# A hybrid encoder layer: three PSUM banks shared by maxima, queries and convolutions, filter taps kept in PSUM, and a modulation that only TensorE sums

## The chip, the cores and the metric

One core of a Trainium2 chip runs the whole layer as one program. The metric is the device time of one execution in microseconds (us); lower is better. TensorE, VectorE, ScalarE, GpSimd and SyncE are called PE, DVE, ACT, POOL and SP, as in the profile.

## The reference, cut to what matters

The layer works on 2048 positions of width 1024 in fp32. Four pieces matter here:

```
mod = silu(c) @ w_ada + b_ada                    # six vectors of 1024: shift, scale, gate, twice
u = x * (1 + sc1) + sh1;  proj = u @ w_in        # feeds attention (8 heads) and the Hyena group
s = q k^T;  p = softmax(s * scale);  o = p v     # per head, 2048 x 2048, no mask
h = (hid @ w3 + b3) * exp(-t * |decay|)          # taps of the two long filters, 2 x 512 channels
y = irfft(rfft(z) * rfft(h))                     # two long convolutions, each followed by a gate
```

The two groups are normalised, joined and multiplied by `w_o`; sixteen SwiGLU experts follow. Matrix products that must be exact to fp32 are made of three fp32r products (`mm3`: high x high, high x low, low x high), so most operands exist as a high part (`hi_of`) and a remainder (`lo_of`).

## The kernel before, in words

The program is written stage by stage, and a scheduler of the compiler orders the instructions of each engine within what data and buffers allow. A buffer pool gives each name a fixed number of buffers; an allocation beyond that number waits until an earlier one has been read for the last time. The PSUM has eight banks of 128 x 512 fp32, and `Banks` hands them out by tag.

Filters (0 to about 240 us). `modulation` loads `w_ada` in sixteen tiles of 128 x 1024 (`w`, five buffers). The first half of the columns is summed over the eight row blocks by PE (L158); of the second half, blocks 0 to 4 are multiplied and added by POOL (L161 to L165), and one product with ones (L170) adds up that sum. `hidden` computes the filters' small network: per block of 512 positions a product, five DVE operations that reduce a sine's argument (L98 to L102), and a sine. `taps(o, q)` then makes 64 tiles of filter taps: `mm3` into a bank of tag `a`, DVE adds the bias and writes SBUF (L307), POOL multiplies by the decay `e` (L308), ACT and DVE split the product (L59 and L65, tile `h`). A second `mm3` per tile (tag `b`) is the first step of the filter's transform. Beside it `ahead` modulates the first half of the input (`inputs`, tiles `ut` and `uT`, L370 to L372) and starts the input projection (tag `mm`).

Projections (240 to 608 us) follow, with the other four modulation vectors, made by DVE in between.

Attention with convolutions (608 to 1900 us). `attention` goes through 32 blocks (8 heads x 4 blocks of 512 queries) of 16 steps. A step makes the scores of 128 keys (tag `s`, three products, L887 to L889), two exponentials by ACT (L892, L893), a remainder by DVE (`el`), a running sum by POOL (L901), and two products with the values (L874, L875, tags `o` and `l`). In the same steps, the maxima of the next block are made: a product of tag `x` (L815) and a DVE reduction (L817), sixteen times; then the row of maxima goes through PE as four transposes (L829, from tile `mz`) and by ACT into the query tile (L830). Only then can the next block's scores start. Queries (`query`) also use tag `x`.

Beside the attention runs `beside`: the values and the keys of the other heads, and then `hyena`, the two long convolutions, in tasks `fwd1` (L652), `spectrum` (L667), `mid` (L694 and L715) and `inv` (L736). All of them use tag `h`, one bank. A credit in the loop at L974 sets how many steps of `beside` are written per step of attention; what is left is written behind it (L979). The bank of one `mid` product is read three times: by DVE (L698) and twice by ACT (L700, L701).

The output projection starts with `prep(0)`: it loads one tile of the attention's output (`at`), one of the convolutions' (`hy`), and the eight tiles of `w_o`, all by SP's queue, whose instructions go in order.

Of the kernel before, what the change touches and what calls it, by code (L numbers as in the profile page):

```python
# [43 lines left out]
def pat(ap, offset, dims):  # L44
    return bass.AP(tensor=ap.tensor, offset=ap.offset + offset, ap=[list(d) for d in dims])
# [3 lines left out]
def hybrid_layer(ctx, tc, I, out):  # L49
# [97 lines left out]
    def modulation(wp, bk, b2):  # L147
        A.activation(sc, vc("c", 0, 8), AF.Silu)
        ps = [bk("sm"), bk("mm"), b2("b"), b2("b")]
        acc = [None, None]  # L150
        for k in range(8):
            for hh in range(2):
                w = wp.tile([128, 1024], F32, name="w")
                SY.dma_start(w, I["w_ada"][0, k * 128:(k + 1) * 128, hh * 1024:hh * 1024 + 1024])
                eng = G if hh and k <= 4 else None
                if eng is None:
                    for j in range(2):
                        T.matmul(ps[hh * 2 + j][0:1], sc[:, k:k + 1], w[:, j * 512:j * 512 + 512],  # L158
                                 start=k == 5 * hh, stop=k == 7 and hh == 0)
                elif k == 0:  # L160
                    G.tensor_scalar(w, w, sc[:, 0:1], 0.0, op0=OP.mult, op1=OP.add)  # L161
                    acc[hh] = w
                else:
                    G.tensor_scalar(w, w, sc[:, k:k + 1], 0.0, op0=OP.mult, op1=OP.add)
                    G.tensor_tensor(acc[hh], acc[hh], w, OP.add)  # L165
            yield
        for hh in range(2):
            for j in range(2):
                if acc[hh] is not None:
                    T.matmul(ps[hh * 2 + j][0:1], ones[:, 0:1], acc[hh][:, j * 512:j * 512 + 512], start=False, stop=True)  # L170
        row = [wp.tile([128, 1024], F32, name="w") for _ in range(2)]
        for j in range(4):
            o = row[j // 2][0:1, j % 2 * 512:j % 2 * 512 + 512]
            if j % 2:
                V.tensor_copy(o, ps[j][0:1])
            else:
                A.activation(o, ps[j][0:1], AF.Copy)
        p = bk("sm")
        for j in range(16):
            T.matmul(p[:, j:j + 1], row[j // 8][0:1, j % 8 * 128:j % 8 * 128 + 128], ones[0:1, 0:1], start=True, stop=True)  # L180
        V.tensor_tensor(sh1, p[:, 0:8], vc("b_ada", 0, 8), OP.add)
        V.scalar_tensor_tensor(s1, p[:, 8:16], 1.0, vc("b_ada", 8, 8), op0=OP.add, op1=OP.add)
        yield
# [41 lines left out]
    def filters(tp, wk, ht, bk):  # L225
# [3 lines left out]
        w3 = ht.tile([128, 2 * CH], F32, name="w3")  # L229
        h1 = ht.tile([128, S], F32, name="h1")  # L230
        negt = tp.tile([128, 32], F32, name="negt")
        b3 = tp.tile([128, 2 * CH], F32, name="b3")
        dec = tp.tile([128, 2 * CH], F32, name="dec")
        SY.dma_start(w1b, I["filt_w1"])
        for b in range(4):
# [6 lines left out]
        for i in range(2):  # L242
            r = slice(i * 64, i * 64 + 64)
            SY.dma_start(dec[r], pat(I["hyena_decay"], i * 1024, [[0, 64], [1, 1024]]))
            SY.dma_start(b3[r], pat(I["filt_b3"], i * 1024, [[0, 64], [1, 1024]]))
        hsh = tp.tile([128, 32, 128], F32R, name="hsh")
        hsl = tp.tile([128, 32, 128], F32R, name="hsl")
        for t in (hsh, hsl):
# [42 lines left out]
        def taps(o, q):  # L291
            oc = slice(o * CH, (o + 1) * CH)
            p = bk("a")
            mm3(p, hsh[:, q, :], hsl[:, q, :], w3h[:, oc], w3l[:, oc], True, True)
            e = wk.tile([128, CH], F32, name="e")
            ex = A.activation(e, dec[:, oc], AF.Exp, scale=negt[:, q:q + 1])
            if len(hs) < 3 and q in (2, 3):
                for d in sines:
                    tc.add_manual_dep(ex.ins, d.ins.name,
                                      mybir.DependencyInfo(mybir.DependencyClass.NoSync, mybir.DependencyReason.DATA),  # L300
                                      reason="one change of the activation table")
            if q == 0:
                hb = wk.tile([128, CH], F32, name="e")
                SY.dma_start(hb[0:1], I["hyena_bias"][0, o:o + 1])
                V.tensor_tensor(b3[0:1, oc], b3[0:1, oc], hb[0:1], OP.add)
            t = wk.tile([128, CH], F32, name="t")
            V.tensor_tensor(t, p, b3[:, oc], OP.add)  # L307
            G.tensor_tensor(t, t, e, OP.mult)  # L308
            if q == 0:
                G.memset(t[64:65, :], 0.0)  # L310
            h = wk.tile([128, 2, CH], F32R, name="h", bufs=3)
            hi_of(A, h[:, 0], t)
            lo_of(V, h[:, 1], t, h[:, 0])
            hs[o, q] = h

        for n, (layer, b) in enumerate(((0, 0), (0, 1), (1, 0), (0, 2), (1, 1), (0, 3), (1, 2), (1, 3))):
            hidden(layer, b)
            if n == 1:
                hi_of(A, w3h, w3)
                lo_of(G, w3l, w3, w3h)  # L320
            yield
        order = list(range(1, 16)) + [0]
        seq = [(o, q2 * 2 + i) for q2 in order for o in range(2) for i in (1, 0)]
# [40 lines left out]
    def inputs(b, xp):  # L364
        for f in range(0, 8, 2):
            xt = xp.tile([128, 2, 512], F32, name="xt")
            SY.dma_start(xt, I["xT"][f * 128:(f + 2) * 128, b * 512:(b + 1) * 512].rearrange("(f p) t -> p f t", p=128))
            for i in range(2):
                t = xp.tile([128, 512], F32, name="ut")
                A.activation(t, xt[:, i], AF.Identity, scale=s1[:, f + i:f + i + 1], bias=sh1[:, f + i:f + i + 1])  # L370
                hi_of(V, uT[b][0][:, f + i], t)
                last_in[0] = lo_of((V if b == 2 else G, V)[i], uT[b][1][:, f + i], t, uT[b][0][:, f + i])  # L372
            yield

    def load_w(job):
# [579 lines left out]
            yield from hyena(pool(hs_, "hc", side="right"), pool(hs_, "hcw", bufs=2, side="right"), bk)  # L955

    with ExitStack() as st:
        at_ = Banks(st, "psT", s=3, x=2, o=1, l=1)
        hb_ = Banks(st, "psH", h=1)
        weight(wk, I["w_kvb"][0])  # L960
        for i in range(2):
            G.dma_start(khs[i][64:96], KR)
        norm_kv(0, at_("x"))
        for b in range(4):
            if b < 3:
                norm_kv(b + 1, at_("x"))
            keys(b, 0, at_("s"), None)
            if b < 2:
                weight(wqs[b], I["w_qb"][0, b * 128:b * 128 + 128])
                norm_q(b, hb_("h"))  # L970
        at = attention(pool(st, "atk"), pool(st, "atw", bufs=2), at_)
        hy = beside(hb_)
        credit = 0.0
        for n, free in enumerate(at):  # L974
            credit += free * (1.5 if n < 12 else 0.8)
            while credit >= 1.0:
                credit -= 1.0
                next(hy, None)
        drive(hy)  # L979
# [748 lines left out]
```

## Time and profile before

| | us |
|---|---|
| three runs, median (lowest to highest) | 3405.52 (3395.53 to 3406.53) |
| the profiled execution, its own time | 3403.19 |
| its span in the trace | 3401.4 |
| PE busy, DVE busy, ACT busy, POOL busy | 3177.4, 2286.6, 1700.0, 1459.6 |

The span is what the trace covers; the execution's own time is 1.8 us longer. The ends of matmuls are modelled, so a busy PE is not a PE at its peak: back to back matmuls of 128 x 512 fp32r start 0.23 us apart while each is shown with some 0.39 us. PEclk is the share of full speed that was granted to TensorE.

### The profile page before, as it was taken

Reading aid. Unit: us, or ns where it says so; the run is one execution under the profiler, and the core shown is the slowest. Engines: PE = TensorE matmul, PEld = TensorE weight load, DVE = VectorE, ACT = ScalarE, POOL = GpSimd, SP = SyncE. Lnnn points to the kernel's source line nnn. Section 1 sums busy time; section 2 is a strip of 40 time slices with the busy share of each in tenths; the row PEclk is TensorE's granted clock in tenths of the full one; section 3 lists DMA queues with packets and bytes.
Section 4 is the critical chain, followed back from the end, with each engine's and each line's share of the span. In section 5 each row is a group of like instructions: output and inputs, shape, how many; then the busy total and the mean of one; then the engine's idle time right before and its main releaser. Section 6 shows DMA issues by size and latency. Waiting matters only on the chain.

```text
span 3401.4 us, 41832 instructions
## 1 busy us (share of the span) xinstructions
PE 3177.4 (93%) x14790; PEld 2466.7 (73%) x14790; DVE 2286.6 (67%) x3528; ACT 1700.0 (50%) x2569; POOL 1459.6 (43%) x1134
## 2 busy tenths in 40 slices
PE   7899999999999999999999799599999999999897
PEld 3667877667677776777777588477788878887676
DVE  7975344786677766776685577776665665665886
ACT  4662222466667666766765343243444444443443
POOL 5650000466777776777786366200100010000564
PEclk8999999699999999999999899799999999999999
DMA  6443352346575764667566543455666666665884
GB/s 195 158 155 114 106 145 81 119 148 179 147 186 144 202 158 146 156 191 197 148 161 216 199 149 118 162 187 184 210 198 198 193 222 217 198 198 186 276 278 163
DMA packets 364794, 594.14 MB, mean 175 GB/s; under 512 B 36092, under 2 KB 189246, under 8 KB 364138
## 3 DMA queue, kind: packets, MB, share of 16 engines
q1 hardware_dynamic: 338137, 528.95, 49.0%
q0 software_dynamic: 26304, 62.00, 7.4%
q8 instruction: 117, 1.92, 0.2%
q14 instruction: 92, 0.75, 0.1%
q10 hardware_dynamic: 144, 0.52, 0.0%
HBM read 438.84 MB, written 152.58 MB: 174 GB/s over the span
## 4 chain that ended last, share of the span: by engine, by line
PE 72%; DVE 11%; DMA 7%; issue 4%; POOL 3%; ACT 3%; SPq 0%; POOLq 0%; DVEq 0%; ACTq 0%
PE g L73 9%; PE g L74 9%; PE g L75 9%; PE s L887 3%; PE s L888 3%; PE mm L75 3%; PE s L889 3%; PE mm L74 3%; PE mm L73 3%; PE x L815 3%; PE o L874 3%; PE l L875 3%; DMA w<-in_w_ada_dram 2%; PE h L736 2%; PE h L652 2%
## 5 line engine op out<-in xcount | busy, mean ns | idle before, releaser
L901 POOL TENSOR_TENSOR acc<-acc,eh 128x512 f32<-128x512 f32 x480 | 615.8, 1283 | 175.9 <-ACT eh L892 155.8
L65 DVE TENSOR_TENSOR wl<-raw,wh 128x2048 fp32r<-128x2048 f32 (+1 forms) x210 | 473.0, 2255 | 224.6 <-ACT wh L59 223.5
L59 ACT ACTIVATE wh<-raw 128x2048 fp32r<-128x2048 f32 x192 | 367.6, 1915 | 440.8 <-PE g L75 337.8
L65 DVE TENSOR_TENSOR el<-s,eh 128x512 fp32r<-128x512 f32 x512 | 348.3, 686 | 175.9 <-ACT s L893 172.3
L892 ACT ACTIVATE eh<-s 128x512 fp32r<-128x512 f32 x512 | 305.1, 596 | 223.5 <-PE s L889 204.8
L817 DVE TENSOR_REDUCE mx<-x 128x1 f32<-128x512 f32 x512 | 341.1, 683 | 111.3 <-PE x L815 108.1
L73 PE MATMUL g<-wh,xh 128*128 128x512 f32 x1024 | 411.9, 403 | 1.3 <-ACT wh L59 0.7
L75 PE MATMUL g<-wh,xl 128*128 128x512 f32 x1024 | 408.2, 399 | 1.0 <-DVE xl L65 1.0
L74 PE MATMUL g<-wl,xh 128*128 128x512 f32 x1024 | 408.8, 399 | 0.0
L1527 POOL DMA_INDIRECT ACC<-ye,idx x30 | 67.9, 2263 | 687.7 <-DVE ye L1518 565.3
L893 ACT ACTIVATE s<-s 128x512 f32<-128x512 f32 x512 | 304.4, 595 | 0.0
L875 PE MATMUL l<-el,vt 128*66 128x512 f32 x512 | 230.0, 452 | 2.3 <-DVE el L65 1.9
L75 PEld LDWEIGHTS g<-wh,xl 128*128 128x128 f32 x1024 | 193.3, 189 | 45.5 <-DVE xl L65 1.4
L73 PEld LDWEIGHTS g<-wh,xh 128*128 128x128 f32 x1024 | 193.4, 189 | 44.8 <-ACT wh L59 1.1
L74 PEld LDWEIGHTS g<-wl,xh 128*128 128x128 f32 x1024 | 193.6, 189 | 43.3 <-DVE wl L65 0.4
L887 PE MATMUL s<-qt,kh 97*128 97x512 f32 x512 | 212.4, 415 | 3.0 <-ACT qt L830 2.0
L815 PE MATMUL x<-kh,qt 96*128 96x512 f32 x512 | 211.3, 441 | 3.9 <-DVE mx L817 2.4
L73 PE MATMUL mm<-uT,wh 128*128 128x512 f32 x512 | 208.1, 408 | 5.3 <-DVE uT L62 5.3
L73 PE MATMUL g<-wh,hh 128*128 128x512 f32 x512 | 206.5, 404 | 4.5 <-ACT hh L59 4.5
L74 PE MATMUL g<-wl,hh 128*128 128x512 f32 x512 | 206.3, 403 | 3.7 <-DVE wl L65 3.7
L74 PE MATMUL mm<-uT,wh 128*128 128x512 f32 x512 | 206.7, 404 | 1.1 <-DVE uT L65 0.7
L75 PE MATMUL mm<-uT,wl 128*128 128x512 f32 x512 | 205.6, 402 | 0.0
(408 smaller groups left out, 6954.6 us busy)
## 6 DMA issues: line engine op xcount, KB each, us to landing
raw<-in_w_gate_dram SPq DMA_DIRECT2D x64, 1024.0 KB, 5.2
raw<-in_w_up_dram SPq DMA_DIRECT2D x64, 1024.0 KB, 7.9
raw<-in_w_down_dram SPq DMA_DIRECT2D x64, 1024.0 KB, 9.7
tc<-F_dr SPq DMA_DIRECT2D x64, 512.0 KB, 6.6
w<-in_w_ada_dram SPq DMA_DIRECT2D x48, 512.0 KB, 4.4
Af<-ev SPq DMA_DIRECT2D x32, 512.0 KB, 2.6
Ad<-tc SPq DMA_DIRECT2D x32, 512.0 KB, 5.2
tc<-Af SPq DMA_DIRECT2D x16, 1024.0 KB, 5.6
```

What stands on the lines that cost most here:

```text
L59: return A.activation(hi, src, AF.Copy)
L65: return eng.tensor_tensor(lo, src, hi.bitcast(F32), OP.subtract)
L73: first = T.matmul(o, wh, xh, start=start, stop=False)
L74: T.matmul(o, wh, xl, start=False, stop=False)
L75: T.matmul(o, wl, xh, start=False, stop=stop)
L815: T.matmul(p, qh[0:96, i * 128:i * 128 + 128], khs[h % 2][0:96, 0, c * 512:c * 512 + 512], start=True, stop=True)
L817: V.tensor_reduce(mx[:, i, c:c + 1], p, axis=AX.X, op=OP.max)
L875: T.matmul(pl[0:66], vt[:, k, 64:130], el, start=k == 0, stop=k == NT - 1)
L887: T.matmul(p, kh[0:97, ks], qh[0:97, :], start=True, stop=False)
L892: A.activation(eh, p, AF.Exp, scale=SCALE)
L893: A.activation(p, p, AF.Exp, scale=SCALE)
L901: G.tensor_tensor(acc, acc, eh.bitcast(F32), OP.add)
```

## The change

Four edits. (1) The modulation's five POOL blocks become PE products like the others. (2) A tile of taps stays in its PSUM bank: the bias is a fourth matmul into the bank (a selecting matrix `sel` times the bias's high and low parts `b3s`), DVE multiplies by the decay in place, and the split reads the bank. (3) Of the input's remainders, all for the first two blocks of positions are made by POOL, all for the last two by DVE. (4) The tag `h` is gone: its bank goes to `x`, which has three, and convolutions, keys, values and the scales of `norm_q` take `x`.

```
@@ modulation
-        acc = [None, None]
...
-                eng = G if hh and k <= 4 else None
-                if eng is None:
-                    for j in range(2):
-                        T.matmul(ps[hh * 2 + j][0:1], sc[:, k:k + 1], w[:, j * 512:j * 512 + 512],
-                                 start=k == 5 * hh, stop=k == 7 and hh == 0)
-                elif k == 0:
-                    G.tensor_scalar(w, w, sc[:, 0:1], 0.0, op0=OP.mult, op1=OP.add)
-                    acc[hh] = w
-                else:
-                    G.tensor_scalar(w, w, sc[:, k:k + 1], 0.0, op0=OP.mult, op1=OP.add)
-                    G.tensor_tensor(acc[hh], acc[hh], w, OP.add)
+                for j in range(2):
+                    T.matmul(ps[hh * 2 + j][0:1], sc[:, k:k + 1], w[:, j * 512:j * 512 + 512], start=k == 0, stop=k == 7)
...
-                    T.matmul(ps[hh * 2 + j][0:1], ones[:, 0:1], acc[hh][:, j * 512:j * 512 + 512], start=False, stop=True)
@@ filters
+        b3s = tp.tile([128, 2 * CH], F32R, name="b3s")
+        sel = tp.tile([128, 128], F32R, name="sel")
+        G.memset(b3, 0.0)
...
-            SY.dma_start(b3[r], pat(I["filt_b3"], i * 1024, [[0, 64], [1, 1024]]))
+        for i in range(4):
+            SY.dma_start(b3[32 * i:32 * i + 1], pat(I["filt_b3"], i % 2 * 1024, [[0, 1], [1, 1024]]))
@@ taps
-            mm3(p, hsh[:, q, :], hsl[:, q, :], w3h[:, oc], w3l[:, oc], True, True)
+            mm3(p, hsh[:, q, :], hsl[:, q, :], w3h[:, oc], w3l[:, oc], True, False)
+            T.matmul(p, sel, b3s[:, oc], start=False, stop=True)
...
-                V.tensor_tensor(b3[0:1, oc], b3[0:1, oc], hb[0:1], OP.add)
-            t = wk.tile([128, CH], F32, name="t")
-            V.tensor_tensor(t, p, b3[:, oc], OP.add)
-            G.tensor_tensor(t, t, e, OP.mult)
+                V.tensor_tensor(p[0:1], p[0:1], hb[0:1], OP.add)
+            V.tensor_tensor(p, p, e, OP.mult)
             if q == 0:
-                G.memset(t[64:65, :], 0.0)
+                V.memset(p[64:65, :], 0.0)
             h = wk.tile([128, 2, CH], F32R, name="h", bufs=3)
-            hi_of(A, h[:, 0], t)
-            lo_of(V, h[:, 1], t, h[:, 0])
+            hi_of(A, h[:, 0], p)
+            lo_of(V, h[:, 1], p, h[:, 0])
@@ inputs
-                last_in[0] = lo_of((V if b == 2 else G, V)[i], uT[b][1][:, f + i], t, uT[b][0][:, f + i])
+                last_in[0] = lo_of((V if b >= 2 else G), uT[b][1][:, f + i], t, uT[b][0][:, f + i])
@@ attention and what runs beside it
-        at_ = Banks(st, "psT", s=3, x=2, o=1, l=1)
-        hb_ = Banks(st, "psH", h=1)
+        at_ = Banks(st, "psT", s=3, x=3, o=1, l=1)
+
+        def hb_(tag):
+            return at_("x")
```

On PE in the filters, this stands before in the middle of the stage (`a` is a tile of taps, `b` the transform's product, `mm` the projection):

```order
L73 MATMUL b_828<-h_778,w1h_759 128x512
L74 MATMUL mm_1743<-uT11_98,wh_529 128x512
L75 MATMUL mm_1743<-uT10_97,wl_530 128x512
L73 MATMUL a_875<-w3h_141,hsh_135 128x512
L74 MATMUL a_875<-w3l_142,hsh_135 128x512
L75 MATMUL a_875<-w3h_141,hsl_136 128x512
L74 MATMUL b_828<-h_778,w1h_759 128x512
L75 MATMUL b_828<-h_778,w1l_760 128x512
```

And in the changed kernel at a like place:

```order
L75 MATMUL b_912<-h_869,w1l_835 128x512
L73 MATMUL a_918<-w3h_151,hsh_145 128x512
L74 MATMUL a_918<-w3l_152,hsh_145 128x512
L75 MATMUL a_918<-w3h_151,hsl_146 128x512
L289 MATMUL a_918<-b3s_121,sel_122 128x512
L73 MATMUL b_930<-h_886,w1h_834 128x512
L74 MATMUL b_930<-h_886,w1h_834 128x512
L75 MATMUL b_930<-h_886,w1l_835 128x512
```

Each tile of taps has a fourth matmul, and nothing else is added to PE there.

On PE at the end of a block of attention, before (`h` is the convolutions' one bank; L829 is the row of maxima that the next scores wait for; the block is the eleventh):

```order
L887 MATMUL s_8852<-qt_7992,kh0_4448 128x512
L888 MATMUL s_8852<-qt_7992,kh0_4448 128x512
L889 MATMUL s_8852<-qt_7992,kh0_4448 128x512
L875 MATMUL l_8587<-el_8816,vt0_4458 66x512
L715 MATMUL h_7797<-y_7497,ivm_5193 128x256 x2
L874 MATMUL o_8586<-eh_8827,vt0_4458 128x512
L815 MATMUL x_8760<-kh0_4448,qt_8371 128x512
L815 MATMUL x_8763<-kh0_4448,qt_8371 128x512
```

In the changed kernel, at the end of the tenth block:

```order
L815 MATMUL x_8360<-kh0_4395,qt_7936 128x512
L815 MATMUL x_8363<-kh0_4395,qt_7936 128x512
L710 MATMUL x_8370<-y_8253,ivm_5137 128x256 x2
L815 MATMUL x_8382<-kh0_4395,qt_7936 128x512
L689 MATMUL x_8404<-ta_8256,zm_5136 128x256 x2
L829 MATMUL x_8427<-ident_60,mz_4534 98x128 x4
L710 MATMUL x_8433<-y_8285,ivm_5137 128x256 x2
L887 MATMUL s_8460<-qt_7936,kh0_4395 128x512
```

Maxima, convolutions (L710 and L689 are L715 and L694 of before) and the row of maxima now take turns on three banks; a bank is taken again after two others.

On SP's queue at the end of the stage, before (L774 and L779 store the last convolution, L1016 loads `w_o`, L1023 loads the first tile of the attention's output, whose last store on this queue stands further ahead):

```order
L774 DMA HY<-tb 128x4x256
L730 DMA tb<-HZ_74 128x4x256
L774 DMA HY<-tb 128x4x256
L779 DMA HY<-tb 128x4x256
L1010 DMA g1b<-gate_83 128x1024
L1016 DMA raw<-in_w_o_dram 128x1024 x8
L1023 DMA at<-AO 128x512
```

And in the changed kernel (L851 stores a block of the attention's output, L769 and L774 the convolution):

```order
L769 DMA HY<-tb 128x4x256 x2
L774 DMA HY<-tb 128x4x256
L1008 DMA g1b<-gate_83 128x1024
L1014 DMA raw<-in_w_o_dram 128x1024 x5
L851 DMA AO<-oo 128x4x64
L1014 DMA raw<-in_w_o_dram 128x1024 x3
L1023 DMA hy<-HY 128x512 x2
L1021 DMA at<-AO 128x512 x2
L851 DMA AO<-oo 128x4x64 x2
```

The last convolution stores and the loads of `w_o` now stand ahead of the attention's last stores. On PE, before, nine groups of `inv` products (L736, four matmuls each) stand behind the last scores; in the changed kernel the last group stands 42 steps of attention ahead of them, and 19 groups of values and keys stand ahead of the first scores, before 11.

## Rows read from the trace of the kernel before

**Rows 1.** The page: the chain that ended last, by engine.

```profile
PE 72%; DVE 11%; DMA 7%; issue 4%; POOL 3%; ACT 3%; SPq 0%; POOLq 0%; DVEq 0%; ACTq 0%
```

**Rows 2.** By stage: busy us of PE, PEld, DVE, ACT, POOL; clock, DMA share, GB/s.

```profile
0.00:60.00 60.00, 38.83 (x75) 10.90 (x76) 43.91 (x54) 24.78 (x37) 35.60 (x27) 0.91 0.63 196
60.00:240.00 180.00, 162.69 (x662) 120.74 (x661) 160.72 (x217) 119.44 (x206) 116.40 (x85) 0.95 0.44 157
608.00:667.00 59.00, 51.18 (x146) 34.99 (x146) 43.34 (x62) 27.84 (x46) 25.01 (x22) 0.57 0.35 98
667.00:1852.00 1185.00, 1124.62 (x4876) 857.10 (x4874) 852.75 (x1391) 806.69 (x1496) 877.18 (x714) 0.98 0.60 166
1852.00:1901.00 49.00, 20.94 (x78) 15.34 (x79) 9.50 (x15) 1.78 (x3) 4.59 (x6) 0.73 0.87 311
```

**Rows 3.** Groups of DVE, 0 to 60 us: count, busy us, mean ns, idle before.

```profile
L101 DVE SCALAR_TENSOR_TENSOR x<-rs_n,x 128x512 f32<-128x512 f32 x16 | 13.3, 839 | 0.1
L99 DVE TENSOR_SCALAR rs_n<-rs_n 128x512 f32<-128x512 f32 x8 | 8.4, 1048 | 0.1
L65 DVE TENSOR_TENSOR hsl<-x,hsh 64x512 fp32r<-64x512 f32 x8 | 8.1, 1007 | 4.2 <-ACT hsh L59 4.1
L102 DVE TENSOR_SCALAR x<-x 128x512 f32<-128x512 f32 x8 | 7.5, 941 | 0.1
L98 DVE TENSOR_SCALAR rs_n<-x 128x512 f32<-128x512 f32 x8 | 5.5, 684 | 3.2 <-ACT x L268 3.2
```

**Rows 4.** Timeline of DVE, 40 to 53 us, where POOL does nothing: start, duration.

```profile
44.04 0.43 DVE L99 TENSOR_SCALAR rs_n<-rs_n 128x512 f32<-128x512 f32 x1
44.50 0.69 DVE L101 SCALAR_TENSOR_TENSOR x<-rs_n,x 128x512 f32<-128x512 f32 x1
...
52.82 0.69 DVE L65 TENSOR_TENSOR hsl<-x,hsh 64x512 fp32r<-64x512 f32 x1
```

**Rows 5.** Timeline of PE: two modulation products in fp32, two products in fp32r.

```profile
28.82 1.02 PE L158 MATMUL sm<-w,sc 128*1 128x512 f32 x2 [1.65 <-DMA w<-in_w_ada_dram]
29.68 1.02 PE L158 MATMUL mm<-w,sc 128*1 128x512 f32 x2
...
593.76 0.39 PE L74 MATMUL mm<-uT,wh 128*128 128x512 f32 x1
593.99 0.39 PE L75 MATMUL mm<-uT,wl 128*128 128x512 f32 x1
```

**Rows 6.** Groups of DVE, 80 to 240 us.

```profile
L65 DVE TENSOR_TENSOR h<-t,h 128x512 fp32r<-128x512 f32 x58 | 63.5, 1098 | 9.9 <-ACT h L59 8.9 <-issue 0.5 <-POOL t L308 0.4
L307 DVE TENSOR_TENSOR t<-a,b 128x512 f32<-128x512 f32 x55 | 37.1, 681 | 2.3 <-PE a L75 0.6
```

**Rows 7.** Waits of PE, 667 to 1852 us: total us, times, longest.

```profile
PE x L829 <- DVE mz L823: 16.0, 16, 3.6
PE h L715 <- ACT zs L701: 10.5, 6, 2.2
PE h L667 <- ACT ta L668: 5.9, 9, 2.0
PE h L652 <- ACT tc L654: 3.6, 7, 0.7
```

**Rows 8.** Groups of POOL and DVE, 667 to 1852 us.

```profile
L901 POOL TENSOR_TENSOR acc<-acc,eh 128x512 f32<-128x512 f32 x479 | 614.5, 1283 | 175.4 <-ACT eh L892 155.4 <-DVE qf L347 2.8 <-POOL acc L901 0.2
L65 DVE TENSOR_TENSOR el<-s,eh 128x512 fp32r<-128x512 f32 x511 | 347.6, 686 | 175.9 <-ACT s L893 172.3 <-PE l L875 1.5 <-PE x L75 0.3
L817 DVE TENSOR_REDUCE mx<-x 128x1 f32<-128x512 f32 x493 | 328.5, 683 | 103.9 <-PE x L815 100.7
```

**Rows 9.** Timeline of SP's queue, 1883 to 1892 us.

```profile
1884.28 5.81 SPq L1016 DMA_DIRECT2D raw<-in_w_o_dram  x8
1891.02 0.33 SPq L1023 DMA_DIRECT2D at<-AO  x1
```

**Rows 10.** Timeline of PE, 1880 to 1901 us.

```profile
1900.71 0.69 PE L1041 MATMUL tr<-ident,at 128*128 128x128 f32 x2 [18.14 <-DMA at<-AO]
```

More of the change, by code (lines that the diff above doesn't have):

```diff
@@ L154, in modulation @@
                 SY.dma_start(w, I["w_ada"][0, k * 128:(k + 1) * 128, hh * 1024:hh * 1024 + 1024])
-                eng = G if hh and k <= 4 else None
-                if eng is None:
-                    for j in range(2):
-                        T.matmul(ps[hh * 2 + j][0:1], sc[:, k:k + 1], w[:, j * 512:j * 512 + 512],
-                                 start=k == 5 * hh, stop=k == 7 and hh == 0)
-                elif k == 0:
-                    G.tensor_scalar(w, w, sc[:, 0:1], 0.0, op0=OP.mult, op1=OP.add)
-                    acc[hh] = w
-                else:
-                    G.tensor_scalar(w, w, sc[:, k:k + 1], 0.0, op0=OP.mult, op1=OP.add)
-                    G.tensor_tensor(acc[hh], acc[hh], w, OP.add)
+                for j in range(2):
+                    T.matmul(ps[hh * 2 + j][0:1], sc[:, k:k + 1], w[:, j * 512:j * 512 + 512], start=k == 0, stop=k == 7)
             yield
-        for hh in range(2):
-            for j in range(2):
-                if acc[hh] is not None:
-                    T.matmul(ps[hh * 2 + j][0:1], ones[:, 0:1], acc[hh][:, j * 512:j * 512 + 512], start=False, stop=True)
         row = [wp.tile([128, 1024], F32, name="w") for _ in range(2)]
@@ L232, in filters @@
         b3 = tp.tile([128, 2 * CH], F32, name="b3")
+        b3s = tp.tile([128, 2 * CH], F32R, name="b3s")
+        sel = tp.tile([128, 128], F32R, name="sel")
+        G.memset(b3, 0.0)
+        G.memset(sel.bitcast(F32), 0.0)
+        for i in range(4):
+            G.memset(sel[32 * i:32 * i + 1, i % 2 * 64:i % 2 * 64 + 64].bitcast(F32), 1.0)
         dec = tp.tile([128, 2 * CH], F32, name="dec")
@@ L244, in filters @@
             SY.dma_start(dec[r], pat(I["hyena_decay"], i * 1024, [[0, 64], [1, 1024]]))
-            SY.dma_start(b3[r], pat(I["filt_b3"], i * 1024, [[0, 64], [1, 1024]]))
+        for i in range(4):
+            SY.dma_start(b3[32 * i:32 * i + 1], pat(I["filt_b3"], i % 2 * 1024, [[0, 1], [1, 1024]]))
         hsh = tp.tile([128, 32, 128], F32R, name="hsh")
@@ L320, in filters @@
                 lo_of(G, w3l, w3, w3h)
+                hi_of(A, b3s, b3)
+                lo_of(G, b3s[64:128], b3[64:128], b3s[64:128])
             yield
```

## The prediction

> **What bounds the kernel now.** I read the page first, and of it the chain that ended last: 72% of it is PE [rows 1]. So a change is worth what it takes from PE's idle time and from the time PE runs at the lower clock, less what it adds to PE. Busy time by stage says where that is [rows 2]. From 0 to 60 us PE is busy 38.8 us of 60. From 60 to 240 us it is busy 162.7 of 180, but DVE is busy 160.7: two engines are near their limit at once. From 608 to 667 us the granted clock is 0.57, near the lower of the two levels (1.2 of 2.4 GHz). In the attention, 667 to 1852 us, PE is busy 1124.6 of 1185: 60.4 us idle, with DVE, ACT and POOL at 68 to 74%. From 1852 to 1901 us it is busy 20.9 of 49, so 28.1 us are idle. The change touches these five stretches and none behind them.
>
> What PE's rows are worth: two fp32r products of 128x512 start 0.23 us apart, and two fp32 products of one row 0.86 us apart [rows 5]. These are the prices of an added product; the busy time of a row is longer.
>
> **The modulation.** POOL loses nine instructions on 128x1024 tiles; PE gains ten products and loses two, so 8 x 0.86 = 6.9 us. They lie in the 21.2 us that PE idles before 60 us [rows 2], and cost nothing there; without that cover, 6.9 us. What is won is DVE's. The sine reductions should cost DVE 16 x 0.69 + 24 x 0.43 and the remainders beside them 8 x 0.69, together 26.8 us by the rows where POOL is idle (I take L98 and L102 at the price of L99) [rows 4]. The five groups took 42.8 us [rows 3], 16.0 us more. They run slower beside POOL's work, most of which is this modulation; its memsets at the start and the first split of weights stay. I take 12 of the 16. ACT's exponentials for the taps wait for the last sine, so the taps start that much earlier. The modulation itself can't end much more than 10 us earlier: its sixteen loads are 8.4 MB, 43 us at the 196 GB/s of this stretch [rows 2]. The smaller of the two counts: **-10 us**, between 0 and -16. Two bias loads of 64 rows become four of one row on SP's queue, ahead of the loads of `w_ada`; the bytes saved (0.5 MB, 2.7 us at that rate) pay for two more issues, so I count nothing.
>
> **The taps.** Each of 64 tiles gets a bias product: 64 x 0.23 = 14.7 us more PE. DVE's add becomes a multiply in place, at the same 0.68 us (bounded by the add that read a bank [rows 6] and the reduction that read one [rows 8]). DVE's split read two SBUF tiles beside POOL at 1.10 us [rows 6]; now it reads a bank and an SBUF tile, as `el` does at 0.69 [rows 8]: 64 x 0.41 = 26 us less DVE. POOL's multiply goes, and with it a step of at least 1.28 us in each tile's chain (POOL's like operation [rows 8]). What is new: a tap's bank is held until DVE's split, through three engines instead of one. With three banks, a product and three readers of some 0.7 us each take about 3 us, against the 8.4 us in which three tiles pass (three times 180 us over 64 tiles), so PE is not made to wait for it in the main. Behind a tap that waits stand the transform and the projection, PE's only other work there.
>
> PE lost 17.3 us of 60 to 240 to waiting, and about 9 us to the clock (5% of 180) [rows 2]. With DVE relieved I take 60% of these 26 us back: 15.6 us, against 14.7 us of added products. **-1, say 0 us**. The ends: all 26 us back gives -12; nothing back gives +15. The remainders that change engine (edit 3) are 4 DVE operations of 0.7 us more at 240 to 300 us, where DVE has room, and count nothing.
>
> The Trainium skill (Perfetto Trace Analysis, Optimizing Scalar/DVE Operations) gives DVE about 125 ns of access overhead in PSUM and 60 ns in SBUF. By that, 64 splits that now read a bank would cost 64 x 0.065 = 4 us more of DVE time, and the result would be up to 4 us later. The trace doesn't bear it out: 0.69 us from two SBUF tiles and 0.686 and 0.681 from a bank [rows 4, 6, 8].
>
> **Three shared banks.** Before, a convolution's product waits until the one bank has been read. The three largest of these waits are 10.5, 5.9 and 3.6 us, 20.0 in all [rows 7]. In the changed order a bank comes again after two other allocations, and what stands between is mostly scores and values. I take three quarters back: **-15 us**, between 0 and -20. The wait for the row of maxima, 16.0 us [rows 7], ends on DVE, not on a bank: it stays.
>
> More follows from the order. Eight more groups of values and keys (24 products, 5.6 us) stand ahead of the first scores, and the convolutions end 42 steps before the last scores instead of behind them. So at the end nothing is left between the last values and the output projection but the closing of a block; `w_o`, whose eight issues took 5.8 us of SP's queue just ahead of the load that PE waited for [rows 9], is loaded by then. Before, PE's first transpose of the projection waited 18.1 us for that load [rows 10], and 28.1 us were idle in that stretch. I leave 5 us for the last block's chain (six or seven operations at 0.69 us): **-23 us**, between -28 and, if the first tile's load is still late, -10. The 15.6 us of convolution products from this stretch are not saved: they move forward.
>
> What that costs: the last 42 steps lose their filler. A step's PE work is six products, 1.4 us, and about 0.2 us for a query and transposes; POOL needs 1.28 and DVE 0.686 + 0.683 = 1.37 us per step, and the block's odd operations [rows 8]. They are close enough that PE will wait. Lower bound 0; upper bound the longest wait for the maxima, 3.6 us [rows 7], at each of three blocks' ends, 11 us. I take **+7 us**, nearer the upper end, as all engines are near their limit there.
>
> Where a wait is new: a product of maxima (L815) can now find its bank held by a `mid` product that three operations read. Behind it on PE stand the next scores, and ACT, DVE and POOL wait for those. That is the first rival below.
>
> **Sum.** -10 + 0 - 15 - 23 + 7 = -41 us against the profiled execution's own 3403.2 us: **3362 us**. That execution is 2.3 us below the median of the three runs; I don't add that.
>
> **Rivals.**
> *The banks give nothing back.* The maxima wait for convolutions as long as the convolutions waited before. Then -15 falls away: 3377 us. For it: a `mid` bank has three readers, two of them on ACT behind exponentials. Against it: maxima waited for their two banks too little to stand among the larger rows [rows 7].
> *The filters gain nothing.* The early stretch is held by the loads of `w_ada`, and PE's added 14.7 and 6.9 us lie on the path with nothing recovered: -10 becomes +22, so 3394 us. For it: PE is already busy 90% from 60 to 240 us [rows 2]. Against it: DVE, just as full, loses 26 us of work.
> *The clock falls where the filler is gone* (slower). In the last 42 steps PE has gaps in each step; if it is granted the lower level there, as from 608 to 667 us, 42 x 1.6 = 67 us of PE work takes twice as long: 3362 + 67 = 3429 us. It decides from 41/67, that is if about 26 of the 42 steps run so. For it: the clock of 0.57 at 87% busy [rows 2]. Against it: 0.98 over the attention, its waits included [rows 2]. The Trainium skill tells of the like (TensorE: Matmul & The Clock Gate, A second HAM failure mode: psum-queue depth-cycling): a PE that idles briefly between groups that cycle through banks is slowed again and again. By it this rival's 3429 us would hold; the attention's 0.98, on banks that cycle already, speaks against it.
>
> **How the numbers follow.** The main case has 0.62 (3336 to 3384 us), the first rival 0.17, the second 0.10, the third 0.07, and 0.04 are left for more gain than that: the best ends together are -16 - 12 - 20 - 28 = -76, 3327 us. The range 3334 to 3391 us holds the main case, the first rival and half of the second, some 0.84. About 0.3% (10 us) is what a measurement of this kernel can tell from no change. Faster by more than that, below some 3393 us: the main case, the first rival, the left-over and nearly half of the second, 0.87. Slower: the third rival and a sum of mishaps, 0.07. The rest, 0.06, is the same.
>
> **What would show it.** Right: the exponentials for the taps start about 12 us earlier, DVE's split of the taps at 0.69 us, the projections end some 10 us earlier; the waits of L715, L667 and L652's products are 5 us or less together; the first transpose of the output projection follows the last values within 6 us, and the attention's span to that point is some 31 us shorter. Wrong: new waits of L815's products of over 10 us, a granted clock well below 0.95 in the last three blocks, a wait for the tile `at` as before, or filters that end no earlier than 240 us.

## The result, and the profile after

The changed kernel took 3362.36 us in the median of four runs (3359.78 to 3367.7), the kernel before 3402.39 (3395.53 to 3406.53): a ratio of 0.9886, interval 0.9869 to 0.9903. 3362 had been predicted. The profiled execution took 3360.98 us, its span is 3359.3.

The chain that ended last, by engine, on the page of the changed kernel [rows 1 of before]:

```profile
PE 75%; DVE 9%; DMA 7%; issue 3%; POOL 2%; ACT 2%; SPq 0%; POOLq 0%; DVEq 0%; ACTq 0%
```

Busy time by stage (columns as in [rows 2]): to the exponentials, the filters, the attention's setup, the attention in two parts (the second has no convolutions), its end:

```profile
0.00:60.00 60.00, 45.03 (x92) 10.91 (x93) 38.50 (x58) 26.17 (x39) 16.69 (x22) 1.00 0.60 188
60.00:225.00 165.00, 161.67 (x713) 128.80 (x712) 118.70 (x199) 114.25 (x202) 31.56 (x30) 0.98 0.47 166
...
596.00:661.00 65.00, 49.20 (x169) 33.02 (x167) 47.20 (x71) 32.32 (x59) 23.83 (x19) 0.76 0.52 159
661.00:1785.00 1124.00, 1067.89 (x4642) 819.42 (x4643) 805.83 (x1307) 754.19 (x1396) 825.05 (x669) 0.98 0.63 178
1785.00:1852.80 67.80, 63.71 (x278) 47.38 (x276) 52.93 (x86) 46.36 (x87) 53.18 (x46) 0.95 0.35 122
1852.80:1859.20 6.40, 2.38 (x12) 2.28 (x12) 3.27 (x5) 2.24 (x4) 6.24 (x7) 0.54 0.00 0
```

Three things are to be seen. In the filters PE is now busy 161.7 of 165 us and DVE only 118.7: PE alone is the limit there. The setup is longer (65 us). And 6.4 us stand where 49 stood [rows 2].

To see where 42 us went, I cut both timelines at the same five instructions: the last product of the filters' transform, the last of the projections, the first scores, the last values (start times), and the first transpose of the output projection. Between them lie the stages:

| us | before | after | difference | predicted |
|---|---|---|---|---|
| filters end at | 233.8 | 223.6 | -10.2 | |
| projections end at | 607.0 | 595.5 | -11.5 | -10 |
| setup of the attention | 54.2 | 65.6 | +11.4 | +5.6 |
| first scores to last values | 1190.1 | 1191.2 | +1.1 | +2.0 |
| last values to output projection | 49.4 | 6.9 | -42.5 | -38.6 |
| the rest of the span | 1500.7 | 1500.1 | -0.6 | 0 |

The predicted column puts the terms where their work lies. The 5.6 us of products that move ahead of the first scores count in the setup and not in the attention; the 15.6 us of convolutions that leave the end count in the attention (-15 + 7 - 5.6 + 15.6 = +2), and the end is -23 - 15.6. Two of these sizes were wrong, and later I use others. The convolutions that leave the end are eight groups, each shown in the trace as eight matmul records. One such group took 1.54 us inside the attention of before (it starts at 1840.34, the next product at 1841.88), so they cost 12.3 us where they now are. And of the groups of values and keys that stand ahead of the first scores, the trace shows seven before and 19 after, not 11 and 19 as the section on the change counts (the first of a group's three products is shown below; four more groups, the first head's keys in tag `s`, are the same in both kernels). Before, then after:

```profile
L73 PE MATMUL h<-wk,ckv 128*128 128x512 f32 x7 | 5.4, 774 | 2.2 <-DVE nm L822 1.5 <-DVE rq L584 0.6
...
L73 PE MATMUL x<-wk,ckv 128*128 128x512 f32 x16 | 8.6, 536 | 3.4 <-DVE mx L812 3.1
L73 PE MATMUL x<-ckv,wk 128*128 128x512 f32 x3 | 1.5, 490 | 0.3 <-DVE vv L65 0.2
```

So 36 products moved and not 24: 8.3 us at the 0.23 us of [rows 5].

PE's largest waits between the first scores and the last values (total us, times, longest) [rows 7 of before]:

```profile
PE x L824 <- DVE mz L818: 30.4, 23, 3.5
PE x L689 <- DMA ta<-Ad: 6.6, 2, 5.0
PE x L824 <- ACT zs L700: 5.0, 2, 2.5
PE x L810 <- DVE mx L812: 4.8, 8, 1.8
PE x L710 <- POOL y L703: 2.0, 1, 2.0
```

The convolutions' waits for ACT are gone from the list, but the wait for the row of maxima (L824, L829 of before), which the prediction left at 16 us, is 30. PE's whole idle time in this stretch is 60.2 us (1124.00 - 1067.89 and 67.80 - 63.71); in the like stretch of before it was 60.2 as well (1190.7 less 1130.5 busy).

### The profile page after: what moved, and what is told of

It reads as the page before. It is cut to its first block, busy times and chain, and to the rows that moved or that the text cites. A ratio compares the mean times of both kernels' runs of the same rounds, so it can differ in the third digit from the quotient of the medians.

```text
span 3359.3 us, 41828 instructions
## 1 busy us (share of the span) xinstructions
PE 3173.9 (94%) x14870; PEld 2473.4 (74%) x14870; DVE 2245.2 (67%) x3526; ACT 1697.3 (51%) x2570; POOL 1352.6 (40%) x1070
## 4 chain that ended last, share of the span: by engine, by line
PE 75%; DVE 9%; DMA 7%; issue 3%; POOL 2%; ACT 2%; SPq 0%; POOLq 0%; DVEq 0%; ACTq 0%
PE g L73 9%; PE g L74 9%; PE g L75 9%; PE mm L75 4%; PE mm L74 4%; PE mm L73 4%; PE s L882 3%; PE s L883 3%; PE s L884 3%; PE o L869 3%; PE l L870 3%; PE x L810 3%; DMA w<-in_w_ada_dram 2%; PE x L710 2%; PE x L731 1%
## 5 line engine op out<-in xcount | busy, mean ns | idle before, releaser
L870 PE MATMUL l<-el,vt 128*66 128x512 f32 x512 | 214.8, 424 | 1.7 <-DVE el L65 1.7
L869 PE MATMUL o<-eh,vt 128*128 128x512 f32 x512 | 215.4, 439 | 0.3 <-ACT eh L887 0.3
```

The source lines that it names most:

```text
L869: T.matmul(po, vt[:, k, 0:128], eh, start=k == 0, stop=k == NT - 1)
L870: T.matmul(pl[0:66], vt[:, k, 64:130], el, start=k == 0, stop=k == NT - 1)
```

## The experiments

The marks of every profiled execution, cut as above. Times are medians; each ratio is against runs of the kernel before beside it on the same chip. "End" is the stretch from the last values to the output projection:

| run | time | ratio to before (interval) | filters end | projections end | setup | attention | end |
|---|---|---|---|---|---|---|---|
| before | 3402.4 | | 233.8 | 607.0 | 54.2 | 1190.1 | 49.4 |
| after | 3362.4 | 0.9886 (0.9869 to 0.9903) | 223.6 | 595.5 | 65.6 | 1191.2 | 6.9 |
| e1, edits 1 to 3 | 3394.2 | 0.9970 (0.9959 to 0.9981) | 222.6 | 597.4 | 52.5 | 1192.1 | 48.7 |
| e2, edit 4 | 3382.3 | 0.9934 (0.9921 to 0.9946) | 232.6 | 607.6 | 63.8 | 1197.6 | 7.8 |
| e3, edit 1 | 3389.7 | 0.9953 (0.9938 to 0.9969) | 226.7 | 599.6 | 52.9 | 1194.7 | 49.8 |
| e4, edit 2 | 3392.5 | 0.9960 (0.9946 to 0.9974) | 231.4 | 602.5 | 52.2 | 1186.1 | 48.5 |
| e5, empty bias product | 3375.0 | 0.9920 (0.9901 to 0.9940) | 236.4 | 604.8 | 62.3 | 1202.1 | 7.8 |
| e6, credit 0.7 | 3394.3 | 0.9972 (0.9958 to 0.9987) | 222.8 | 594.7 | 65.8 | 1188.9 | 48.8 |
| e7, early credit 0.8 | 3358.4 | 0.9863 (0.9837 to 0.9888) | 223.1 | 595.4 | 58.2 | 1195.7 | 7.8 |
| e8, no early POOL | 3357.0 | 0.9867 (0.9845 to 0.9890) | 215.5 | 591.7 | 65.5 | 1190.3 | 7.0 |
| e9, maxima early | 3351.6 | 0.9854 (0.9838 to 0.9871) | 222.3 | 595.3 | 66.1 | 1173.9 | 7.8 |
| e10, e7 and e8 | 3353.1 | 0.9863 (0.9843 to 0.9883) | 216.3 | 586.2 | 58.6 | 1191.4 | 7.8 |
| e11, before with e9 | 3412.9 | 1.0026 (1.0015 to 1.0037) | 232.2 | 605.2 | 54.9 | 1174.9 | 76.3 |
| e12, e7, e8 and e9 | 3336.9 | 0.9803 (0.9791 to 0.9816) | 216.7 | 589.3 | 58.6 | 1180.8 | 7.8 |

The marks are those of one execution each, and not all of these lie at their kernel's median: e6's took 8.7 us more, e3's 7.6 us more, e9's 4.3 us less. Nor does the attention's length repeat well. Its source is the same in before, e1, e3 and e4, and these differ by 8.6 us there; the same, too, in after, e2, e5 and e8, and these differ by 11.8, the longest (e5) at a granted clock of 0.97, the others at 0.98. So less than some 10 us in that column shows nothing by itself. PE's idle time there is steadier: 60.1 to 62.6 us in the first four, 60.1 to 64.3 in the others.

### One edit at a time: e1 to e4

e1 puts the single bank back into the changed kernel; e2 changes only that in the kernel before:

```
-        at_ = Banks(st, "psT", s=3, x=3, o=1, l=1)
...
-        def hb_(tag):
-            return at_("x")
+        at_ = Banks(st, "psT", s=3, x=2, o=1, l=1)
+        hb_ = Banks(st, "psH", h=1)
```

> The changed kernel with the fourth edit undone: the convolutions have their own single bank again, the three early edits stay. My theory: the early stretch and the banks add up without touching each other; the projections end some 11 us earlier than before and nothing else moves: -11 us, 3391 us, and PE's last stretch of the attention is idle for 28 us as before. Rival (the early gain depends on what follows): the time saved is lost again where the attention begins, whose setup took 11.6 us longer in the changed kernel; then 0 us, 3402.

> The kernel before with the fourth edit alone. My theory: the setup of the attention, the attention and its end together give about -30 us, 3372 us, nearly all of it because the convolutions end some 42 steps ahead of the last scores, so that w_o is loaded and the first transpose of the output projection follows the last values within 7 us. Rival (the banks give nothing back and the end was won only because the early stretch was shorter): -10 to -15 us.

e1 gave 3394.2, e2 3382.3. The early edits are worth 10 us without the banks; the banks alone 21 us, less than the 30 I expected: the end is 42 us shorter as it should be, but the setup takes 9.6 and the attention 7.5 us more (the latter within the spread above). The bank alone brings the convolutions ahead of the last values: the credit is the same in before, after, e1 and e2, yet with one bank (before, e1) 64 of their records stand behind the last values, with shared banks (e2, after) none. By their intervals the two ratios multiplied (0.9904) still touch that of the whole change.

e3 and e4 take over `modulation` alone and `filters` (with `taps`) alone; their diffs are those of edits 1 and 2 above. Edit 3 has no run of its own; it is in e1.

> The kernel before with the first edit alone: all of the modulation's first half on PE. My theory (the prediction's step): DVE's reductions of the sines run faster without POOL beside them, the exponentials for the taps start 6 to 12 us earlier, and the projections end 6 to 10 us earlier: 3393 to 3396 us. Rival (the taps set the end of the filters, since DVE is full from 60 to 240 us): the earlier start is lost there and the time is that of before within 3 us.

> The kernel before with the second edit alone: taps stay in their bank, the bias goes through PE. The prediction's step: 14.7 us more of PE against 26 us less of DVE, 0 us net, 3402. Rival one (the early gain of the changed kernel is mostly this edit's): the projections end some 8 to 11 us earlier, 3391 to 3394. Rival two (PE was the bound already): up to +14 us, 3416.

Both helped: 3389.7 and 3392.5. Edit 1 ends the filters 7 us earlier (its exponentials start at 44.18, 10.6 us earlier), edit 2 some 2.5 us, though its exponentials start 1 us later. Together in e1 the filters end 11 us earlier, a little more than the sum, but in time e1 is ahead of neither, and e3's and e4's ratios multiplied (0.9913) lie below its interval. One loss can be seen: the modulation's last product of a tile `w` starts at 53.00 in e3, but at 59.41 in e1, hardly earlier than before (59.98). On PE's queue the hidden layer's first product (L260) stands ahead of the modulation's; it starts at 12.72 in e3 and at 18.73 in e1 and in the changed kernel. e8 comes back to this.

### What a product costs in the filters: e5

```
+        zer = tp.tile([128, 128], F32R, name="zer")
...
-            T.matmul(p, sel, b3s[:, oc], start=False, stop=True)
+            T.matmul(p, sel, b3s[:, oc], start=False, stop=False)
+            T.matmul(p, zer, b3s[:, oc], start=False, stop=True)
```

> The changed kernel with a second, empty bias product (a matrix of zeros) in each of the 64 tiles of taps: 64 x 0.23 = 14.7 us more PE, nothing else. My theory, from the trace of the changed kernel (PE 161.7 of 165 us busy from 60 to 225 us): PE now sets the end of the filters, so +11 to +15 us, 3373 to 3377. Rival (the prediction's step: DVE sets the pace there and a product more per tile lies beside its work): +4 us or less, 3366.

3375.0: 12.6 us for 14.7 us of products, and the filters end 12.8 us later. PE sets the end of the filters, and a bias product costs nearly its full price there.

### Where the convolutions end: e6

```
-            credit += free * (1.5 if n < 12 else 0.8)
+            credit += free * (1.5 if n < 12 else 0.7)
```

> The changed kernel with a credit of 0.7 in place of 0.8: three shared banks, but nine groups of the last convolution stand behind the last scores, as in the kernel before. My theory: the time of the end comes back, 41.8 us more from the last values to the output projection less the 12 us of products that leave the attention: +29 us, 3391. Rival (it is the sharing itself that gave the time, wherever the convolutions end): +10 us or less, 3372.

3394.3, as my theory had it, and the same time as e1 with its single bank. Its profiled execution, 3403.0 us, is the slowest of the eleven, but the mark of the end is clear: it takes 48.8 us again. PE's timeline there:

```profile
1866.09 3.69 PE L731 MATMUL x<-tc,ta 128*128 128x256 f32 x16 [2.40 <-issue]
1873.33 6.40 PE L731 MATMUL x<-tc,ta 128*128 128x256 f32 x16 [3.54 <-issue]
1898.15 1.08 PE L1039 MATMUL tr<-ident,at 128*128 128x128 f32 x4 [18.43 <-DMA at<-AO]
```

And of PE's waits from the first scores to the last values, the first row:

```profile
PE x L824 <- DVE mz L818: 50.9, 25, 3.9
```

Three shared banks show no gain over e1's single one here, since the convolutions still end behind the attention. What the 12.3 us of products that left the attention gave back is open. In this execution the attention became 2.3 us shorter than in the changed kernel, and PE's idle time there rose from 60.1 to 68.9 us, most of it in the wait for the row of maxima (50.9 us). But the execution is 8.7 us above its median, and by the medians (31.9 us more than the changed kernel, with 41.9 us more at the end) some 10 us came back, if nothing else differs. So a part of PE's work there lay beside a wait; how large a part, this run does not tell.

### The setup: e7

```
-            credit += free * (1.5 if n < 12 else 0.8)
+            credit += free * (0.8 if n < 12 else 0.8)
```

> The changed kernel with a credit of 0.8 from the start (1.5 in the first twelve steps before): fewer values stand ahead of the first scores, and the convolutions end 32 steps ahead of the last. My theory: of the 11.6 us by which the attention's setup grew, 5.6 us are products that only moved and about 6 us are waits of values and maxima for each other's banks; the waits go, the products come back later: -3 to -6 us, 3356 to 3359. Rival (the setup is set by the chain of queries, keys and maxima, and the waits lie beside it): within 2 us of the changed kernel.

3358.4 (-4.0, with an interval that reaches to no change). The setup became 7.4 us shorter, the attention, which got the products back, 4.5 longer (within the spread). The size fits the theory, the reason does not. Eight groups of values and keys, 24 products, left the setup, and PE's busy time there fell by 5.6 us (49.7 to 44.1), its idle time only by 1.8 (15.9 to 14.1; before the change it was 7.8). The values' wait for a bank of the maxima fell from 3.1 to 0.8 us, but the largest wait, of a product of the norms' scales (L563) for a bank that DVE reads, stayed (4.8 and 4.7 us). So most of the new waits are still there, and the gain in time is at the limit of what can be told.

### The sines beside POOL: e8

```
-                lo_of(G, w3l, w3, w3h)
+                lo_of(V, w3l, w3, w3h)
...
-                lo_of(G, b3s[64:128], b3[64:128], b3s[64:128])
+                lo_of(V, b3s[64:128], b3[64:128], b3s[64:128])
```

> The changed kernel with the remainders of w3 and b3 (5.1 us of POOL between 11 and 16 us) made by DVE. My theory: three DVE operations beside them took 2.83, 2.56 and 1.41 us where 0.69, 0.43 and 0.69 are usual, so they cost the chain of sines some 5 to 6 us; DVE's own two operations cost 2.4; the exponentials for the taps start about 3 to 4 us earlier and the filters end 2 to 4 us earlier: 3358 to 3360. Rival (the loads of w_ada set the end of this stretch): no change, 3362.

3357.0, 5.4 us less (the intervals of the two ratios overlap), and not in the way I wrote. The timeline of the changed kernel, two rows of DVE and two of POOL, 10 to 17 us (start, duration):

```profile
11.22 2.83 DVE L101 SCALAR_TENSOR_TENSOR x<-rs_n,x 128x512 f32<-128x512 f32 x1
13.98 2.56 DVE L99 TENSOR_SCALAR rs_n<-rs_n 128x512 f32<-128x512 f32 x1
...
11.08 2.43 POOL L65 TENSOR_TENSOR w3l<-w,w3h 128x1024 fp32r<-128x1024 f32 x1 [0.18 <-POOL sel L225]
13.59 2.67 POOL L65 TENSOR_TENSOR b3s<-b,b3s 64x1024 fp32r<-64x1024 f32 x1
```

Each of the two DVE operations ends 0.3 to 0.5 us behind the POOL operation beside it, as if it had waited for that one's end. The Trainium skill (SBUF — State Buffer, section SBUF: two separate sides) says that DVE and GpSimd share a pair of ports that one of them locks for a whole instruction; these rows agree. In e8 the same operations take 0.69 and 0.42 us. (The 1.41 us that I had expected to shorten is a row of two operations, 17.93 us, behind POOL's; nothing delayed it.) Yet the exponentials start only 1 us earlier (47.76). What moved is PE's queue. In the changed kernel:

```profile
18.73 2.07 PE L260 MATMUL a<-h,w2b 128*128 128x512 f32 x2 [10.70 <-ACT h L266]
20.59 1.92 PE L258 MATMUL a<-feats,w1b 66*128 66x512 f32 x2
22.44 1.86 PE L155 MATMUL sm<-w,sc 128*1 128x512 f32 x2
...
60.44 1.88 PE L155 MATMUL b<-w,sc 128*1 128x512 f32 x4
```

And in e8:

```profile
14.24 1.87 PE L155 MATMUL sm<-w,sc 128*1 128x512 f32 x2 [6.39 <-DMA w<-in_w_ada_dram]
15.90 1.91 PE L155 MATMUL mm<-w,sc 128*1 128x512 f32 x2
17.74 1.77 PE L260 MATMUL a<-h,w2b 128*128 128x512 f32 x2
...
51.59 1.88 PE L155 MATMUL b<-w,sc 128*1 128x512 f32 x4
```

The product of the hidden layer (L260) that waits 10.7 us for the sine stood on PE ahead of the modulation's products; the five buffers `w` stayed full behind it, and the last modulation product came at 60.44, no earlier than before the change (59.98). In e8 the compiler's order has the modulation's first products ahead of it. The modulation ends 8.9 us earlier, the input projection, which needs it, starts 8.6 us earlier (67.92, 76.55 in the changed kernel), and the filters end 8.1 us earlier. How much of the 5.4 us is this order and how much the ports, one run doesn't split.

### What sets a block's length: e9 and e11

The end of a block in the changed kernel, on DVE, then one row of POOL, then PE:

```profile
888.04 0.69 DVE L830 TENSOR_TENSOR acc<-l,acc 1x512 f32<-1x512 f32 x1
888.76 0.68 DVE L831 TENSOR_TENSOR osb<-o,osb 64x512 f32<-64x512 f32 x1
889.37 0.67 DVE L693 TENSOR_TENSOR pr<-x,tc 128x512 f32<-128x512 f32 x1
889.97 0.67 DVE L812 TENSOR_REDUCE mx<-x 128x1 f32<-128x512 f32 x1
...
891.47 1.16 DVE L818 COPY mz<-nm 128x4 f32<-128x4 f32 x1
...
891.35 1.26 POOL L701 TENSOR_TENSOR zs<-zs,tc 128x512 f32<-128x512 f32 x1 [2.35 <-ACT zs L696]
...
887.67 0.59 PE L810 MATMUL x<-kh,qt 96*128 96x512 f32 x1
...
892.78 0.61 PE L824 MATMUL x<-ident,mz 128*98 128x128 f32 x4 [3.52 <-DVE mz L818]
```

The last product of maxima is ready at 888.3; three other operations stand ahead of its reduction on DVE, one of them the convolution's (L693); the copy of the row takes 1.16 us, beside the convolution's operation on POOL; the row is copied by 892.6, and until then PE waits.

In the kernel before, this stretch was no shorter. PE at the end of a like block, and DVE's copy of the row:

```profile
1511.20 0.39 PE L815 MATMUL x<-kh,qt 96*128 96x512 f32 x1
1513.79 1.13 PE L715 MATMUL h<-y,ivm 128*128 128x256 f32 x4 [2.20 <-ACT zs L701]
1515.25 0.64 PE L829 MATMUL x<-ident,mz 128*98 128x128 f32 x4 [0.33 <-DVE mz L823]
...
1514.75 0.45 DVE L823 COPY mz<-nm 128x4 f32<-128x4 f32 x1
```

A convolution's product waits 2.20 us for its one bank, but DVE had the row ready only at 1515.2. Over 31 block ends, from the end of the last product of maxima to the row's transposes, the mean is 3.18 us before and 3.15 us after, and PE is idle 49.2 us in these stretches before and 40.8 after, of some 60 in the whole attention. Of the 20.0 us of waits for the bank [rows 7], 19.8 lie in them. So when the bank's waits went, PE came to the row earlier and waited there.

e9 makes the maxima earlier within a block:

```
-                for j in itertools.islice(maxes, 2 if k in (2, 6, 11) else 1):
+                for j in itertools.islice(maxes, 2 if k in (1, 3, 5, 7) else 1):
```

> The changed kernel with the four steps of a block that make two maxima moved from steps 2, 6 and 11 (and what was left behind them) to steps 1, 3, 5 and 7, so that a block's sixteenth maximum is made in step 11. My theory: the chain of maxima, row and query sets when a block can follow the other, and the time that the convolutions no longer wait for their bank went into it (the row of maxima was waited for 30 us, 16 before); made earlier, the waits for the row fall to 15 us or less and the attention gets 8 to 15 us shorter: 3347 to 3354. Rival (the waits for the row lie beside other limits of the block): the waits move to the scores, the values or the convolutions, and the time stays within 4 us of 3362.

3351.6, 10.7 us less (the intervals of the two ratios just touch); the attention is 17 us shorter in the profile, which is the fastest of the four executions, and the row's wait is nearly gone (same view as above, of e9):

```profile
PE x L689 <- DMA ta<-Ad: 10.9, 3, 7.7
PE x L810 <- DVE mx L812: 6.4, 10, 1.1
PE x L824 <- DVE mz L818: 5.2, 8, 0.9
```

PE's idle time in the attention fell from 60.1 to 50.8 us, and in the stretches before the row to 18.2; some of it moved to other waits. The other 8 us of the 17 are busy time, at a granted clock of 0.99 instead of 0.98.

e11 makes the same edit in the kernel before:

> The kernel before with the maxima moved as in the run on the changed kernel, and nothing else: one bank for the convolutions. My theory: here the convolutions' waits for their bank and the waits for the row share the limit; the row's 16 us fall to 6 or less, but the bank's waits stay and three more groups of products stand behind the last scores: 0 to -6 us, 3396 to 3402, so that the shared banks are worth some 45 to 50 us where the maxima are early, and 40 where they are late. Rival (the maxima's chain sets the pace in both kernels alike, whatever the banks): -10 us, 3392.

3412.9, slower by 0.26%, which neither theory had. Its attention is 15.2 us shorter, but the end is 26.9 us longer. PE there:

```profile
1840.60 1.91 PE L715 MATMUL h<-y,ivm 128*128 128x256 f32 x4 [0.83 <-ACT zs L701]
1843.29 2.05 PE L715 MATMUL h<-y,ivm 128*128 128x256 f32 x4 [0.78 <-ACT tb L717]
...
1891.36 1.99 PE L736 MATMUL h<-tc,ta 128*128 128x256 f32 x8 [1.64 <-DVE tb L741]
1911.28 1.11 PE L1041 MATMUL tr<-ident,at 128*128 128x128 f32 x4 [17.93 <-DMA at<-AO]
```

Here most of the attention's gain is work that moved: 52 records of the convolutions more than before stand behind the last values, about 10 us at the price above (0.19 us each), while PE's idle time in the attention fell only from 60.1 to 55.5 us. Behind it they cost more, since nearly each group waits for the last one's reader. I had also expected the row's wait to fall from 16 us; it is 16.1 over a like stretch. With the maxima early, the change with shared banks is worth some 60 us (3412.9 to 3351.6), with the maxima late 40.

### The edits that helped, together: e10 and e12

> The changed kernel with the early credit of 0.8 and with the remainders of w3 and b3 on DVE, the two single edits that came out 4.0 and 5.4 us below it. My theory: they touch different stretches and add up, -9 us, 3353. Rival (what the filters win is lost in the setup of the attention, where the loads of the weights come late): -5 us or less, 3357 or more.

> The changed kernel with all three edits that helped: the early credit of 0.8, the remainders of w3 and b3 on DVE, the maxima in earlier steps. My theory: three stretches, three gains that add up: 3353 - 10.7 = 3342. Rival (with the maxima early the attention is held by something else, so that the values and keys that the credit moves into it cost their full time): 3348 or more.

e10: 3353.1, what the two single gains add up to (3362.4 - 4.0 - 5.4 = 3353.0; the intervals are wider than that agreement). e12: 3336.9, somewhat better than the sum: 2.0% below the kernel before, and 25 us below the changed kernel's median.

## Why the prediction was right

The time was right to 0.4 us, and so near a hit is luck: the end gave more than forecast, the banks and the setup less. Point by point, with 12.3 us of convolutions that move into the attention and 8.3 us of values and keys that move out of it (predicted, then measured):

- **The modulation (-10) and the taps (0): -11.5 at the end of the projections.** The size was right. Of the mechanism, half: the sines' five groups [rows 3] cost DVE 34.1 us instead of 42.8, 8.7 less and not 12. The exponentials start at 48.73, 6 us earlier and not 12; with edit 1 alone they start 10.6 us earlier (e3), so edit 2 costs some 5 us there. That it is its work on POOL (`b3s`, memsets) is not shown: e8, which moves two of these operations to DVE, wins only 1 us. And the modulation itself did not end earlier, for PE's queue (e8).
- **The bias products lie beside DVE's work.** This step failed in its form. DVE's split took 0.684 us as predicted, and PE's waits for it, 13.2 us in the filters before, fell to 0.8. So PE became the limit, and each bias product costs its price (e5). The net of 0 held because more came back than the 60% I took: idle fell from 17.3 us [rows 2] to 3.3 and the clock rose from 0.95 to 0.98.
- **The banks (-15) and the missing filler (+7), -8 together: -2.9** (1.1 - 12.3 + 8.3, uncertain by the attention's spread of some 10 us). The idle time says it better: 60.2 us in the attention of both kernels. The step that failed is to book the 20 us of waits for the bank as time that comes back. They went, but nearly all of them lay beside the chain from the last product of maxima through DVE to the row, which is as long as before (see e9 and e11). "It stays", said of the row, was true of that chain, not of the wait. PE's wait for the row rose from 16.0 to 30.4 us (14.5 to 16.0 in the four executions with one bank and late maxima, 30.4 to 30.8 in four with shared banks: after, e2, e5 and e8). So the first rival's outcome, that the banks give nothing back, is right for this term as far as the idle time tells; its mechanism had a small part, for products of maxima waited 4.8 us for a bank that DVE read, and the row 5.0 us for one that a `mid` product held. The filler's price was right in kind: in the last 67.8 us PE is idle 4.1 us.
- **The end (-23): -42.5 + 12.3 = -30.2.** Right in mechanism (the fourth edit alone does it, e2), too small: 5 us were left for the last block's chain, and no other idle was counted; the end of before also held 64 records of convolutions at a granted clock of 0.73 [rows 2], which cost more there than the 12.3 us that they cost now. The 15.6 us of the prediction were too many. The first transpose follows the last values by 6.9 us from start to start.
- **The setup (nothing but the moved 5.6): +11.4.** The count of 11 groups before was wrong, and 8.3 us are moved products at the price of the full clock; the other 3.1 were not foreseen. PE's idle time there rose from 7.8 to 15.9 us, with new waits for the shared banks, while the granted clock rose from 0.57 to 0.76. e7 takes back 7.4 us of the setup, mostly products and not waits.
- **Rivals.** That the filters gain nothing is refuted by e1, the lower clock at the end by the rows: 0.95 without convolutions, PE busy 94%. The rule of the Trainium skill named with that rival (TensorE: Matmul & The Clock Gate, A second HAM failure mode: psum-queue depth-cycling) did not come to bear: these stretches cycle through banks with short waits, and the granted clock stays at 0.95 and more there.

In short, -11.5, -2.9, -30.2, +3.1 for the setup and -0.6 behind it make -42.1, against -41. Behind the end lies what e6 showed: the gain of the fourth edit hangs on the convolutions being done before the last values. Shared banks are the means here (e1 and e2); that a higher credit with one bank could not do the same, no run tested. As a gain in waits of their own the banks are not to be seen.

Open is why e1 gains less time than e3 and e4 together, what sets the setup's length, and how much of PE's work in the attention lies beside its waits. The attention's 1.1 us by itself is no more than noise.

## What to carry to other kernels

Before the waits for a buffer are booked as a gain, find the chain that sets the length of a block, mark its two ends in the trace and see whether the waits lie between them; if they do, as 19.8 of 20.0 us did here, they only move to another row. A stage's length in one profiled execution can be off by more than the effect that is sought: compare executions of the same code first, and look at idle time beside length. What runs beside a long stage should be done before that stage's last step, so that its last stores and the next stage's loads lie beside work. After an engine has been relieved, the next limit should be measured with an empty instruction (e5), before more is moved to it.

## What the runs showed of the hardware that was not expected

Two DVE operations of 0.69 and 0.43 us took 2.83 and 2.56 us beside POOL operations of 2.43 and 2.67 us and ended 0.3 to 0.5 us after them. A DVE copy of 128x4 elements, 0.17 us in the median of 32, took 1.16 us at the block's end shown above, beside a POOL operation that ended with it, and 2.45 at most; in the kernel before the same copies took 0.43 us in the median and 4.15 at most. And in the setup the granted clock was 0.76 after the change, 0.57 before, with PE busy a smaller share of it (49.2 of 65.0 us, against 51.2 of 59.0 [rows 2]).
